# A streaming-encoder layer: gate row spread over the up-projection tiles, first weight products and DVE pages ahead of it

## The chip, the cores and the metric

The kernel runs on one core of one Trainium2 chip. Its metric is the device time of one execution in microseconds (us), the median of several runs. Five engines with an instruction stream each work side by side: TensorE (PE, matmuls), VectorE (DVE), ScalarE (ACT), GpSimd (POOL) and SyncE (SP). In this kernel SP issues the DMA transfers, in the order of its own stream: a transfer whose wait is not met holds all later ones back. A matmul reads its operands from on-chip memory (SBUF) and sums into one of the banks of PSUM; DVE and ACT read PSUM.

## The reference, cut to what matters

One layer on 1024 tokens of width 1024, all in float32. The attention half ends in an output projection with a gated residual; the channel half is a gated MLP of inner width 2816 with a causal convolution of width 3:

```
mod = silu(c) @ w_ada + b_ada;  sh_a, sc_a, g_a, sh_m, sc_m, g_m = split(mod, 6)
...
mixed = concat([o_mla, o_ca]) @ w_out
x = x + g_a * mixed
h = rmsnorm(x) * (1 + sc_m) + sh_m
u = causal_dwconv(h @ w_up, conv_w, conv_b)
gate, val = split(u, 2)
x = x + g_m * ((silu(gate) * val) @ w_down)
```

The row `g_m`, the last sixth of `mod`, is needed only where the down-projection's weights are multiplied by it.

## The kernel before, in words

A float32 product is made of three faster matmuls: each operand is split into a high part (ACT copies it to a shorter format) and a low part (DVE or POOL subtracts the high part from the original), and high x high, high x low and low x high are summed. Such a pair of 128x512 pieces is called a page when it belongs to the activations. The helpers `hi_of` (L75) and `lo_of` (L82) record all of these splits, so their rows all carry those two lines and are told apart by their tiles.

The part around the change has three stages.

*Output projection* (L873 to L901). For each of 8 blocks of 128 tokens: load `ol` (the attention output, transposed), the residual `x1` and a partial sum `pa`, split `ol`, 24 matmuls into a PSUM tile `op`, then DVE adds `pa` (L887), multiplies by the attention gate (L888); the residual add (L889) is on DVE for odd blocks and on POOL for even ones. The sum is stored (L890), squared and summed on ACT (L891), its inverse root made on POOL (L115, L116), and the block scaled in place on POOL (`scale_pool`, L71), which must wait until the store has read it. The tile `x1` has 6 buffers, so the loads of blocks 6 and 7 wait until PE has transposed blocks 0 and 1 for the last time.

*Pages.* `mod_T` turns four scaled blocks on PE (L858) and modulates them on ACT (L860). The first half of the tokens gives the pages `b11` and `b21` (four each). After block 7 the second half is done (L905 to L917): for each of four k, two `mod_T`, four subtractions on DVE (L908, L910, L913, L915) and five pages `t3`, `t1`, `b22`, `t2`, `t4`. ACT makes the five high parts; POOL makes the low parts of `t3`, `b22` and `t4`, DVE those of `t1` and `t2`. These pages, with the combinations of weights in `ff_tile`, are Winograd's form of a 2x2 block product: 7 products in place of 8.

*Up-projection* (`ff_tile`, L974), 22 tiles. A tile loads two raw weight pieces of 512 KB (`raw`, 3 buffers), forms on DVE the combinations of its quarters (L990, L992, L993, L1000), splits seven 128x512 pieces `wa` to `wg` (ACT high, POOL low, 7 buffers `ws`), and runs 7 products of 12 matmuls (L962 to L964), in the order wa with `b11`, wb with `b21`, wc with `t3`, wd with `t2`, we with `t1`, wf with `t4`, wg with `b22`. DVE adds the products up out of PSUM (L995 to L1002), then come the convolution (ACT L969, DVE L970, L971), the SiLU gate and a store. After tile 2 stands `gate_row` (L937): eight loads of 512 KB of `w_ada` through the same three `raw` buffers, eight multiply-adds over 128x1024 on DVE (L942, L944), the bias row (L455), two matmuls with a matrix of ones that sum over the partitions (L456) and two copies to `gmbc`.

*Down-projection* (from L1011): two halves of 22 steps of 24 matmuls, with weights multiplied by `gmbc` (L1024).

The order inside each engine's stream is not that of the source: the framework that builds the program reorders by its own estimate of times, engine by engine, and takes waits from the buffers.

Of the kernel before, what the change touches and what calls it, by code (L numbers as in the profile page):

```python
# [23 lines left out]
P = 128  # L24
D = 1024
# [37 lines left out]
def layer_kernel(ctx, tc, I, out):  # L63
# [809 lines left out]
    for t in range(NT):  # L873
        lo = gb.tile([P, 4, P], F32R, name=f"ol{t}", tag="ol", bufs=3)
        hi = gb.tile([P, 4, P], F32R, name=f"oh{t}", tag="oh", bufs=3)
        sp.dma_start(f32(lo[:]), oT_d[0:4, :, t * P:(t + 1) * P].rearrange("k p t -> p k t"))
        hi_of("a", hi[:], f32(lo[:]))
        lo_of("p", lo[:], f32(lo[:]), hi[:])
        x1 = tb.tile([P, D], F32, name=f"x1_{t}", tag="x1", bufs=6)
        sp.dma_start(x1[:], I["x"][t * P:(t + 1) * P, :])  # L880
# [6 lines left out]
        dve.tensor_tensor(pa[:], pa[:], pt[:], op=ADD)  # L887
        dve.tensor_tensor(pa[:], pa[:], gabc[:], op=MUL)  # L888
        (dve if t % 2 else pool).tensor_tensor(x1[:], x1[:], pa[:], op=ADD)  # L889
        sp.dma_start(x1_d[t], x1[:])  # L890
        act.activation(pa[:], x1[:], AF.Square, accum_out=ss2[:, t:t + 1])  # L891
        rsqrt_mean(r2[:, t:t + 1], ss2[:, t:t + 1], D)
        xn2[t] = x1
        scale_pool(x1[:], x1[:], r2[:, t:t + 1])
        if t % 4 == 3:
            h = t // 4
            if h == 0:
                for k in range(ND):
                    v0[k] = mod_T(k, 0)
                    bpage("b11" if k < 4 else "b21", k % 4, v0[k], "v" if k % 2 else "p")  # L900
# [4 lines left out]
    for k in range(4):  # L905
        b12, b22 = mod_T(k, 1), mod_T(k + 4, 1)
        t3 = tb.tile([P, 512], F32, name=f"t3_{k}", tag="v", bufs=11)
        dve.tensor_tensor(t3[:], b22[:], b12[:], op=SUB)  # L908
# [6 lines left out]
        dve.tensor_tensor(v0[k + 4][:], v0[k + 4][:], b22[:], op=SUB)  # L915
        bpage("t4", k, v0[k + 4], "p")
    tbp.__exit__(None, None, None)  # L917
    psB.__exit__(None, None, None)

    mlp = tc.tile_pool(name="mlp", bufs=1, side="right", reuse_waits="tile")
    mp = mlp.__enter__()
    psC = tc.tile_pool(name="psC", bufs=1, space=PSUM, reuse_waits="tile")
    ps3 = psC.__enter__()
    MB = {"raw": 3, "s": 5, "ws": 7, "c": 2, "u": 2}

    def mt(tag, shape, name, dt=F32):
        return mp.tile(list(shape), dt, name=name, tag=tag, bufs=MB[tag])  # L930

    def bank(tag, name, n=1):
        return ps3.tile([P, n * 512], F32, name=name, tag=tag, bufs=1)


    def gate_row():
        acc = mt("u", [P, D], "adacc5")  # L937
        for k in range(ND):
            w = mt("raw", [P, D], f"adaw5_{k}")
            sp.dma_start(w[:], I["w_ada"][k * P:(k + 1) * P, 5 * D:6 * D])  # L940
            if k == 0:
                dve.tensor_scalar(acc[:], w[:], cs[:, 0:1], None, op0=MUL)  # L942
            else:
                dve.scalar_tensor_tensor(acc[:], w[:], cs[:, k:k + 1], acc[:], op0=MUL, op1=ADD)  # L944
        for h in range(2):
            pt = bank("G", f"p_gm{h}")
            gate_bcast(pt[:], acc[:, h * 512:(h + 1) * 512], 5 * D + h * 512, 512, lambda n: mt("s", [P, 512], n))
            act.activation(gmbc[:, h * 512:(h + 1) * 512], pt[:], AF.Copy)

    def split(src, nm):
        w = mt("ws", [P, 2, 512], nm, F32R)
        hi_of("a", w[:, 0], src)
        lo_of("p", w[:, 1], src, w[:, 0])
        return w

    def product(pt, w, b):
        for k in range(4):
# [3 lines left out]
            pe.matmul(pt, sh, pg[:, 1], start=False, stop=False)  # L963
            pe.matmul(pt, sl, pg[:, 0], start=False, stop=(k == 3))  # L964

    def conv(c, ch):
# [3 lines left out]
        dve.scalar_tensor_tensor(u[:, 1:], c[:, :S - 1], pk[:, cv + 1:cv + 2], u[:, 1:], op0=MUL, op1=ADD)  # L970
# [3 lines left out]
    def ff_tile(j):  # L974
        raw = []
        for i in range(2):
            r = mt("raw", [P, D], f"wu{i}_{j}")
            sp.dma_start(r[:], I["w_up"][i * NF + j].rearrange("p k m -> p (k m)"))
            raw.append(r)
        a11, a12, a21, a22 = raw[0][:, :512], raw[0][:, 512:], raw[1][:, :512], raw[1][:, 512:]  # L980
        p1, p5, p6 = (bank(n, f"{n}_{j}") for n in ("p1", "p5", "p6"))
        p27, p34 = bank("p27", f"p27_{j}", 2), bank("p34", f"p34_{j}", 2)

        c = mt("c", [P, 7, 512], f"c{j}")
        product(p1[:], split(a11, f"wa{j}"), "b11")
        act.activation(c[:, 0], p1[:], AF.Copy)
        product(p27[:, :512], split(a12, f"wb{j}"), "b21")

        t3 = mt("s", [P, 512], f"ws3_{j}")
        dve.tensor_tensor(t3[:], a11, a21, op=SUB)  # L990
        product(p27[:, 512:], split(t3[:], f"wc{j}"), "t3")
# [3 lines left out]
        dve.tensor_tensor(c[:, 6], c[:, 0], p6[:], op=ADD)  # L995
        dve.tensor_tensor(c[:, 0::5][:, 0:2], c[:, 0::6][:, 0:2], p27[:].rearrange("p (a b) -> p a b", a=2), op=ADD)
# [121 lines left out]
```

## Time and profile before

| | us |
|---|---|
| median of 3 runs | 1493.73 (1491.92 to 1497.59) |
| the profiled execution, its own time | 1497.56 |
| its span in the profile | 1495.8 |
| PE busy | 1283.1 |
| DVE busy | 1037.7 |
| POOL busy | 841.8 |
| ACT busy | 617.5 |

Rows of the timeline give the start and the duration in us, the engine, the source line, the operation, what it writes `<-` what it reads, the shape, the count of merged instructions, and in brackets how long the engine had been idle before and what ended that. Rows of a table by stretches give, for each stretch, its length, each engine's busy time with the count of instructions, the granted TensorE clock (1.00 is full speed), the share of the DMA engines and the rate moved. Matmuls overlap: their spacing, not the printed duration, is their price.

### The profile page before, as it was taken

To read this page: it belongs to the slowest core of one execution; us is meant where nothing else is said; L and a number is where in the kernel's file an instruction comes from. 1 tells how busy PE (TensorE), PEld (TensorE's weight loads), DVE (VectorE), ACT (ScalarE), POOL (GpSimd) and SP (SyncE) were. 2 spreads that over 40 slices of the span, in tenths; PEclk is the share of its full clock that TensorE was granted. 3 is DMA by queue.
4 is the path that set the end of the run, shared out by engine and by line. 5 is a ranking of instruction groups with operands and counts; after the bars stand their busy time and mean duration, and the time that the engine had idled before them with its cause. 6 is when DMAs were issued, how large, how long until landed. Compare 5 with 4: busy or idle time off the path is not lost.

```text
span 1495.8 us, 20236 instructions
## 1 busy us (share of the span) xinstructions
PE 1283.1 (86%) x6836; PEld 1063.9 (71%) x6836; DVE 1037.7 (69%) x1710; ACT 617.5 (41%) x1190; POOL 841.8 (56%) x860
## 2 busy tenths in 40 slices
PE   3859989998968788876829769999999999999997
PEld 2759868976747666655617558888888887887885
DVE  6864786466768768863576658887787788556553
ACT  4454353343546545532444224444444443332331
POOL 4264453373799845443766146665565555665663
PEclk9979988998878899987958979999999999999999
DMA  7323656464512668778411242222222234446442
GB/s 275 134 70 73 135 121 143 116 134 102 124 49 53 145 144 167 163 156 287 149 74 57 71 143 82 85 85 85 85 85 84 77 129 169 148 148 234 154 141 99
DMA packets 217443, 185.94 MB, mean 124 GB/s; under 512 B 147958, under 2 KB 182906, under 8 KB 216316
## 3 DMA queue, kind: packets, MB, share of 16 engines
q1 hardware_dynamic: 217340, 184.66, 43.0%
q8 instruction: 54, 0.88, 0.2%
q14 instruction: 49, 0.40, 0.1%
HBM read 121.17 MB, written 28.84 MB: 100 GB/s over the span
## 4 chain that ended last, share of the span: by engine, by line
PE 48%; DMA 16%; DVE 13%; POOL 12%; issue 7%; ACT 2%; SPq 1%; DVEq 0%; POOLq 0%; ACTq 0%
PE p L964 7%; PE p L962 7%; PE p L963 7%; POOL wds L82 4%; DMA aw<-w_ada 4%; DMA PTm<-hlm 3%; PE sc L658 3%; PE dnp L1034 2%; PE dnp L1036 2%; PE dnp L1035 2%; DVE adacc L243 1%; DMA wu<-w_up 1%; PE ipv L150 1%; DVE aacc L430 1%; PE pvc L716 1%
## 5 line engine op out<-in xcount | busy, mean ns | idle before, releaser
L82 POOL TENSOR_TENSOR wds<-wd,wds 128x512 fp32r<-128x512 f32 x88 | 153.5, 1763 | 100.2 <-ACT wds L75 100.2
L1034 PE MATMUL dnp<-wds,g 128*128 128x512 f32 x308 | 119.9, 391 | 4.3 <-DVE xo L1042 2.4
L1024 DVE TENSOR_TENSOR wd<-wd,gmbc 128x1024 f32<-128x1024 f32 x44 | 69.4, 1578 | 77.7 <-DMA wd<-w_down 77.7
L1035 PE MATMUL dnp<-wds,g 128*128 128x512 f32 x308 | 119.7, 389 | 0.0
L1036 PE MATMUL dnp<-wds,g 128*128 128x512 f32 x308 | 118.5, 390 | 0.5 <-DVE g L82 0.5
L75 ACT ACTIVATE wds<-wd 128x512 fp32r<-128x512 f32 x88 | 54.6, 624 | 152.0 <-PE dnp L1036 149.6
L71 POOL TENSOR_SCALAR hlm<-Pm,rim 128x512 f16<-128x512 f32 (+4 forms) x88 | 61.7, 704 | 71.6 <-DMA PTm<-hlm 53.9
L703 DVE SCALAR_TENSOR_TENSOR hlm<-Pm,rim,hlm 128x512 f16<-128x512 f32 (+4 forms) x88 | 69.7, 795 | 31.7 <-POOL hlm L71 31.4
L71 POOL TENSOR_SCALAR hlc<-Pc,ric 128x640 f16<-128x640 f32 (+2 forms) x64 | 45.5, 713 | 77.9 <-DVE ric L686 38.7
L82 POOL TENSOR_TENSOR wc<-ws,wc 128x512 fp32r<-128x512 f32 x22 | 50.8, 2311 | 64.9 <-ACT wc L75 64.9
L82 POOL TENSOR_TENSOR wa<-wu,wa 128x512 fp32r<-128x512 f32 x22 | 35.9, 1633 | 91.1 <-ACT wa L75 91.1
L970 DVE SCALAR_TENSOR_TENSOR u<-c,pk,u 128x1023 f32<-128x1023 f32 x44 | 75.6, 1725 | 4.1 <-ACT u L969 4.1
L82 DVE TENSOR_TENSOR g<-gr,g 128x512 fp32r<-128x512 f32 x44 | 70.9, 1613 | 8.8 <-ACT g L75 8.8
L683 ACT ACTIVATE Pc<-sc,mc 128x640 f32<-128x640 f32 (+2 forms) x64 | 42.2, 659 | 83.6 <-DVE mc L673 66.9
L658 PE MATMUL sm<-mk,mq 96*128 96x512 f32 (+3 forms) x288 | 70.2, 378 | 7.0 <-ACT Pm L683 6.5
L716 PE MATMUL pvm<-PTm,vt 128*128 128x128 f16 x576 | 50.6, 242 | 29.4 <-DMA PTm<-hlm 25.3
L658 PE MATMUL sc<-k,q 64*128 64x512 f32 (+3 forms) x288 | 69.8, 370 | 5.6 <-ACT Pc L683 3.7
L430 DVE SCALAR_TENSOR_TENSOR aacc<-aw,cs,aacc 128x256 f32<-128x256 f32 x84 | 45.5, 541 | 41.8 <-DMA aw<-w_ada 41.2
L716 PEld LDWEIGHTS <-vt 128*128 128x128 f16 x576 | 41.2, 110 | 42.8 <-issue 40.0
L1034 PEld LDWEIGHTS dnp<-wds,g 128*128 128x128 f32 x308 | 57.8, 188 | 18.0 <-DVE xo L1042 3.3
L1036 PEld LDWEIGHTS dnp<-wds,g 128*128 128x128 f32 x308 | 57.8, 188 | 13.5 <-DVE g L82 1.4
L971 DVE SCALAR_TENSOR_TENSOR u<-c,pk,u 128x1022 f32<-128x1022 f32 x44 | 66.8, 1554 | 0.0
(352 smaller groups left out, 4350.8 us busy)
## 6 DMA issues: line engine op xcount, KB each, us to landing
wu<-w_up SPq DMA_DIRECT2D x44, 512.0 KB, 3.5
wd<-w_down SPq DMA_DIRECT2D x44, 512.0 KB, 3.5
aw<-w_ada SPq DMA_DIRECT2D x96, 128.0 KB, 2.3
g_d<-u SPq DMA_DIRECT2D x22, 512.0 KB, 2.6
gr<-g_d SPq DMA_DIRECT2D x44, 256.0 KB, 3.1
x<-x SPq DMA_DIRECT2D x16, 512.0 KB, 7.4
adaw<-w_ada_a SPq DMA_DIRECT2D x8, 1024.0 KB, 4.9
wq_r<-w_qk SPq DMA_DIRECT2D x32, 128.0 KB, 2.4
```

Source lines behind the costliest of these rows:

```text
L71: pool.tensor_scalar(o, i, s, 1.0, op0=MUL, op1=MUL)
L82: (pool if eng == "p" else dve).tensor_tensor(o, i, f32(hi), op=SUB)
L658: last = pe.matmul(s[:, c:c + w], qpg[rs_, a, q], kpgs[kh][rs_, b, ko:ko + w], start=(a == 0 and b == 0), stop=(a == 1))
L703: dve.scalar_tensor_tensor(hl[:, w:2 * w], pp, ri[:], hl[:, :w], op0=MUL, op1=SUB)
L716: last = pe.matmul(u.pv[:, c], u.vst(j), mov, start=(x == 0), stop=(x == len(todo) - 1))
L962: pe.matmul(pt, sh, pg[:, 0], start=(k == 0), stop=False)
L963: pe.matmul(pt, sh, pg[:, 1], start=False, stop=False)
L964: pe.matmul(pt, sl, pg[:, 0], start=False, stop=(k == 3))
L970: dve.scalar_tensor_tensor(u[:, 1:], c[:, :S - 1], pk[:, cv + 1:cv + 2], u[:, 1:], op0=MUL, op1=ADD)
L1034: pe.matmul(pts[t][n], sh, w[n][:, 0], start=(j == 0), stop=False)
L1035: pe.matmul(pts[t][n], sh, w[n][:, 1], start=False, stop=False)
L1036: pe.matmul(pts[t][n], sl, w[n][:, 0], start=False, stop=(j == NF - 1))
```

## The change

Four things are changed.

1. *Gate row.* `gate_row` becomes a generator that is advanced once after each tile from tile 2 on. It loads one block of 128 rows of `w_ada` as two 128x512 pieces into the five buffers `s` one step ahead, and sums it straight into `gmbc` with two DVE instructions per block (tiles 3 to 10). After two more steps come the bias, the two matmuls and the copies.
2. *First tile's head.* The loads of tile 0's weights and its first two products (wa with `b11`, wb with `b21`) are put ahead of the second half's pages. They sum into a PSUM tile of the output projection, and ACT copies both to a `raw` buffer `p12_0`. For this the buffers `raw` and a new pair `w2` (wa and wb of every tile, and `g` of the down-projection) are allocated in a pool of their own before the pages; `ws` shrinks from 7 to 5.
3. *Low parts.* All 20 low parts of the second half's pages are made by DVE (before: 8 by DVE, 12 by POOL).
4. *Blocks 6 and 7.* `x1` has 8 buffers in place of 6; for these two blocks the residual add and the scaling are on DVE.

In the streams that result, SP issues both weight loads of tile 0 ahead of the last load of `w_out` and of the residual loads, and the residual loads of blocks 6 and 7 directly behind the other six. PE's stream has tile 0's two products among the transposes after block 7's matmuls, and DVE's has the 36 instructions of the second half's pages in a row, with the first weight combination of tile 0 behind them.

```diff
-        x1 = tb.tile([P, D], F32, name=f"x1_{t}", tag="x1", bufs=6)
+        x1 = tb.tile([P, D], F32, name=f"x1_{t}", tag="x1", bufs=8)
...
-        (dve if t % 2 else pool).tensor_tensor(x1[:], x1[:], pa[:], op=ADD)
+        (dve if t % 2 or t > 5 else pool).tensor_tensor(x1[:], x1[:], pa[:], op=ADD)
...
-        scale_pool(x1[:], x1[:], r2[:, t:t + 1])
+        (dve if t > 5 else pool).tensor_scalar(x1[:], x1[:], r2[:, t:t + 1], 1.0, op0=MUL, op1=MUL)
...
-    MB = {"raw": 3, "s": 5, "ws": 7, "c": 2, "u": 2}
+    mlp0 = tc.tile_pool(name="mlp0", bufs=1, side="right", reuse_waits="tile")
+    mp = {"a": mlp0.__enter__()}
+    MB = {"raw": 3, "w2": 2, "s": 5, "ws": 5, "c": 2, "u": 2}
...
+    def ff_head(j, p1, p2):
+        raw = []
+        for i in range(2):
+            r = mt("raw", [P, D], f"wu{i}_{j}")
+            sp.dma_start(r[:], I["w_up"][i * NF + j].rearrange("p k m -> p (k m)"))
+            raw.append(r)
+        product(p1, split(raw[0][:, :512], f"wa{j}", "w2"), "b11")
+        product(p2[:, :512], split(raw[0][:, 512:], f"wb{j}", "w2"), "b21")
+        return raw, p1, p2
+
+    pre = ps2.tile([P, 1024], F32, name="op_0", tag="op", bufs=3)
+    head = ff_head(0, pre[:, :512], pre[:, 512:])
+    pc = mt("raw", [P, D], "p12_0")
+    act.activation(pc[:], pre[:], AF.Copy)
+    head = (head[0], pc[:, :512], pc[:, 512:])
     for k in range(4):
...
-        bpage("t3", k, t3, "p")
+        bpage("t3", k, t3, "v")
...
-        bpage("b22", k, b22, "p")
+        bpage("b22", k, b22, "v")
...
-        bpage("t4", k, v0[k + 4], "p")
+        bpage("t4", k, v0[k + 4], "v")
...
     def gate_row():
-        acc = mt("u", [P, D], "adacc5")
+        def load(k):
+            ws = [mt("s", [P, 512], f"adaw5_{k}{h}") for h in range(2)]
+            for h in range(2):
+                c = 5 * D + h * 512
+                sp.dma_start(ws[h][:], I["w_ada"][k * P:(k + 1) * P, c:c + 512])
+            return ws
+
+        nxt = load(0)
+        yield
         for k in range(ND):
-            w = mt("raw", [P, D], f"adaw5_{k}")
-            sp.dma_start(w[:], I["w_ada"][k * P:(k + 1) * P, 5 * D:6 * D])
+            cur, nxt = nxt, load(k + 1) if k + 1 < ND else None
+            for h in range(2):
+                acc = gmbc[:, h * 512:(h + 1) * 512]
...
+                    dve.scalar_tensor_tensor(acc, cur[h][:], cs[:, k:k + 1], acc, op0=MUL, op1=ADD)
+            yield
+        yield
...
+    gr_gen = gate_row()
     for j in range(NF):
-        ff_tile(j)
-        if j == 2:
-            gate_row()
+        if j:
+            head = ff_head(j, bank("p1", f"p1_{j}")[:], bank("p27", f"p27_{j}", 2)[:])
+        ff_tile(j, head)
+        if j >= 2:
+            next(gr_gen, None)
```

More of the change, by code (lines that the diff above doesn't have):

```diff
@@ L904, in layer_kernel, with split @@
     hpools.append(bp2.__enter__())
[L905 to L908, printed above, removed]
-        bpage("t3", k, t3, "p")
-        dve.tensor_tensor(b12[:], b12[:], v0[k][:], op=SUB)
-        bpage("t1", k, b12, "v")
-        bpage("b22", k, b22, "p")
-        dve.tensor_tensor(b22[:], b22[:], b12[:], op=SUB)
-        bpage("t2", k, b22, "v")
-        dve.tensor_tensor(v0[k + 4][:], v0[k + 4][:], b22[:], op=SUB)
-        bpage("t4", k, v0[k + 4], "p")
[L917 to L926, printed above, removed]
-    MB = {"raw": 3, "s": 5, "ws": 7, "c": 2, "u": 2}
-    def mt(tag, shape, name, dt=F32):
[L930 to L936, printed above, removed]
-        acc = mt("u", [P, D], "adacc5")
-        for k in range(ND):
-            w = mt("raw", [P, D], f"adaw5_{k}")
-            sp.dma_start(w[:], I["w_ada"][k * P:(k + 1) * P, 5 * D:6 * D])
[L941 to L953, printed above, removed]
+    mlp0 = tc.tile_pool(name="mlp0", bufs=1, side="right", reuse_waits="tile")
+    mp = {"a": mlp0.__enter__()}
+    MB = {"raw": 3, "w2": 2, "s": 5, "ws": 5, "c": 2, "u": 2}
+    def mt(tag, shape, name, dt=F32):
+        return mp["a" if tag in ("raw", "w2") else "b"].tile(list(shape), dt, name=name, tag=tag, bufs=MB[tag])
+    def split(src, nm, tag="ws"):
+        w = mt(tag, [P, 2, 512], nm, F32R)
         hi_of("a", w[:, 0], src)
@@ new lines, in layer_kernel @@
+    head = ff_head(0, pre[:, :512], pre[:, 512:])
+    pc = mt("raw", [P, D], "p12_0")
+    act.activation(pc[:], pre[:], AF.Copy)
+    head = (head[0], pc[:, :512], pc[:, 512:])
+    for k in range(4):
+        b12, b22 = mod_T(k, 1), mod_T(k + 4, 1)
+        t3 = tb.tile([P, 512], F32, name=f"t3_{k}", tag="v", bufs=11)
+        dve.tensor_tensor(t3[:], b22[:], b12[:], op=SUB)
+        bpage("t3", k, t3, "v")
+        dve.tensor_tensor(b12[:], b12[:], v0[k][:], op=SUB)
+        bpage("t1", k, b12, "v")
+        bpage("b22", k, b22, "v")
+        dve.tensor_tensor(b22[:], b22[:], b12[:], op=SUB)
+        bpage("t2", k, b22, "v")
+        dve.tensor_tensor(v0[k + 4][:], v0[k + 4][:], b22[:], op=SUB)
+        bpage("t4", k, v0[k + 4], "v")
@@ new lines, in layer_kernel, with bank, gate_row @@
+    tbp.__exit__(None, None, None)
+    psB.__exit__(None, None, None)
+    mlp = tc.tile_pool(name="mlp", bufs=1, side="right", reuse_waits="tile")
+    mp["b"] = mlp.__enter__()
+    psC = tc.tile_pool(name="psC", bufs=1, space=PSUM, reuse_waits="tile")
+    ps3 = psC.__enter__()
+    def bank(tag, name, n=1):
+        return ps3.tile([P, n * 512], F32, name=name, tag=tag, bufs=1)
+    def gate_row():
+        def load(k):
[6 more added lines that the diff above has]
+        yield
+        for k in range(ND):
+            cur, nxt = nxt, load(k + 1) if k + 1 < ND else None
+            for h in range(2):
+                acc = gmbc[:, h * 512:(h + 1) * 512]
+                if k == 0:
+                    dve.tensor_scalar(acc, cur[h][:], cs[:, 0:1], None, op0=MUL)
+                else:
+                    dve.scalar_tensor_tensor(acc, cur[h][:], cs[:, k:k + 1], acc, op0=MUL, op1=ADD)
+            yield
+        yield
+        for h in range(2):
+            acc = gmbc[:, h * 512:(h + 1) * 512]
+            pt = bank("G", f"p_gm{h}")
+            gate_bcast(pt[:], acc, 5 * D + h * 512, 512, lambda n: mt("s", [P, 512], n))
+            act.activation(acc, pt[:], AF.Copy)
@@ L972, in conv, with ff_tile @@
         return u
[L974 to L979, printed above, removed]
+    def ff_tile(j, head):
+        raw, p1, p2 = head
         a11, a12, a21, a22 = raw[0][:, :512], raw[0][:, 512:], raw[1][:, :512], raw[1][:, 512:]
-        p1, p5, p6 = (bank(n, f"{n}_{j}") for n in ("p1", "p5", "p6"))
-        p27, p34 = bank("p27", f"p27_{j}", 2), bank("p34", f"p34_{j}", 2)
+        p5, p6, p34 = bank("p5", f"p5_{j}"), bank("p6", f"p6_{j}"), bank("p34", f"p34_{j}", 2)
         c = mt("c", [P, 7, 512], f"c{j}")
-        product(p1[:], split(a11, f"wa{j}"), "b11")
-        act.activation(c[:, 0], p1[:], AF.Copy)
-        product(p27[:, :512], split(a12, f"wb{j}"), "b21")
+        if j:
+            act.activation(c[:, 0], p1, AF.Copy)
         t3 = mt("s", [P, 512], f"ws3_{j}")
         dve.tensor_tensor(t3[:], a11, a21, op=SUB)
-        product(p27[:, 512:], split(t3[:], f"wc{j}"), "t3")
+        p7 = p2[:, 512:] if j else bank("p1", "p7_0")[:]
+        product(p7, split(t3[:], f"wc{j}"), "t3")
         dve.tensor_tensor(a21, a21, a22, op=ADD)
@@ L994, in ff_tile @@
         product(p6[:], split(a11, f"wd_{j}"), "t2")
-        dve.tensor_tensor(c[:, 6], c[:, 0], p6[:], op=ADD)
-        dve.tensor_tensor(c[:, 0::5][:, 0:2], c[:, 0::6][:, 0:2], p27[:].rearrange("p (a b) -> p a b", a=2), op=ADD)
+        dve.tensor_tensor(c[:, 6], c[:, 0] if j else p1, p6[:], op=ADD)
+        if j:
+            dve.tensor_tensor(c[:, 0::5][:, 0:2], c[:, 0::6][:, 0:2], p2[:].rearrange("p (a b) -> p a b", a=2), op=ADD)
+        else:
+            dve.tensor_tensor(c[:, 0], p1, p2, op=ADD)
+            dve.tensor_tensor(c[:, 5], c[:, 6], p7, op=ADD)
         product(p5[:], split(a21, f"we{j}"), "t1")
@@ L1008, in ff_tile @@
         sp.dma_start(g_d[j], ug[:])
+    gr_gen = gate_row()
     for j in range(NF):
-        ff_tile(j)
-        if j == 2:
-            gate_row()
+        if j:
+            head = ff_head(j, bank("p1", f"p1_{j}")[:], bank("p27", f"p27_{j}", 2)[:])
+        ff_tile(j, head)
+        if j >= 2:
+            next(gr_gen, None)
     for h in range(2):
@@ L1027, in layer_kernel @@
             sp.dma_start(gr[:], g_d[j][:, h * 512:(h + 1) * 512])
-            g = mt("ws", [P, 2, 512], f"g{h}_{j}", F32R)
+            g = mt("w2", [P, 2, 512], f"g{h}_{j}", F32R)
             hi_of("a", g[:, 0], gr[:])
@@ L1046, in layer_kernel @@
     mlp.__exit__(None, None, None)
+    mlp0.__exit__(None, None, None)
     bp2.__exit__(None, None, None)
```

## The prediction

> **What bounds the kernel now.** I read the page's sums first, then a table by stretches, then the timeline at the two stretches where PE is idle, then the periodic part.
>
> ```profile
> span 1495.8 us, 20236 instructions
> PE 1283.1 (86%) x6836; PEld 1063.9 (71%) x6836; DVE 1037.7 (69%) x1710; ACT 617.5 (41%) x1190; POOL 841.8 (56%) x860
> ```
>
> ```profile
> core 0: us, PE busy (x) PEld busy (x) DVE busy (x) ACT busy (x) POOL busy (x), PEclk, DMA share, GB/s
> 684.00:744.00 60.00, 53.70 (x221) 42.35 (x222) 29.68 (x24) 19.41 (x34) 35.98 (x31) 0.90 0.59 212
> 744.00:787.00 43.00, 9.18 (x37) 6.10 (x37) 31.77 (x30) 23.52 (x40) 27.32 (x21) 0.54 0.23 86
> 849.00:874.00 25.00, 0.71 (x1) 0.50 (x2) 18.34 (x17) 4.58 (x5) 0.79 (x1) 0.59 0.50 170
> 874.00:1239.00 365.00, 365.00 (x1600) 300.90 (x1598) 292.25 (x244) 153.76 (x212) 221.67 (x137) 1.00 0.25 88
> ```
>
> From 874 to 1239 PE never rests: tiles 3 to 21 are bound by PE. It rests in two places: 744 to 787 (second half's pages) and 849 to 874 (gate row). The change touches both.
>
> ```profile
> 810.69 0.39 PE L962 MATMUL p<-b,wa 128*128 128x512 f32 x1
> 829.73 0.39 PE L962 MATMUL p<-b,wa 128*128 128x512 f32 x1
> 848.54 0.39 PE L964 MATMUL p<-b,wg 128*128 128x512 f32 x1
> 857.78 0.75 DVE L942 TENSOR_SCALAR adacc<-adaw,cs 128x1024 f32<-128x1024 f32 x1
> 863.61 3.92 DVE L944 SCALAR_TENSOR_TENSOR adacc<-adaw,cs,adacc 128x1024 f32<-128x1024 f32 x3 [2.43 <-DMA adaw<-w_ada]
> 868.38 1.28 DVE L944 SCALAR_TENSOR_TENSOR adacc<-adaw,cs,adacc 128x1024 f32<-128x1024 f32 x1 [0.85 <-DMA adaw<-w_ada]
> 872.50 0.63 ACT L75 ACTIVATE wa<-wu 128x512 fp32r<-128x512 f32 x1 [16.12 <-DMA wu<-w_up]
> 873.29 2.08 PE L456 MATMUL p_gm<-adacc,ones 128*128 128x512 f32 x2 [24.36 <-DVE adacc L455]
> 880.83 1.02 PE L456 MATMUL p_gm<-adacc,ones 128*128 128x512 f32 x2
> 881.29 0.80 PE L964 MATMUL p<-b,wb 128*128 128x512 f32 x1
> 896.22 0.39 PE L962 MATMUL p<-b,wa 128*128 128x512 f32 x1
> ```
>
> A tile takes 829.73 - 810.69 = 19.04 us, 0.227 per matmul. After tile 2 (848.54 + 0.23 = 848.77) PE waits 24.36 us for DVE's sum, which waits for `w_ada`; tile 3's weights come behind those eight loads (ACT idle 16.12).
>
> **The change part by part.**
>
> *Gate row.* From the end of tile 2 to the first matmul of tile 4 pass 896.22 - 848.77 = 47.45 us, 28.4 more than a tile. What stays on PE is the two sums over partitions: the second took 881.29 - 880.83 = 0.46 at full speed; with weight loads I put 1.2 for both. Gain 27.2. What it now costs lies on DVE and SP in tiles 3 to 10:
>
> ```profile
> 980.00:1200.00 220.00, 220.00 (x973) 182.15 (x972) 177.06 (x152) 92.79 (x126) 132.19 (x82) 1.00 0.23 82
> L970 DVE SCALAR_TENSOR_TENSOR u<-c,pk,u 128x1023 f32<-128x1023 f32 x23 | 41.8, 1816 | 0.0
> 1022.47 2.94 POOL L82 TENSOR_TENSOR wc<-ws,wc 128x512 fp32r<-128x512 f32 x1 [4.03 <-ACT wc L75]
> 1034.94 0.39 PE L962 MATMUL p<-t,wc 128*128 128x512 f32 x1
> 1029.20 0.33 SPq L978 DMA_DIRECT2D wu<-w_up  x1
> 1032.72 0.69 DVE L990 TENSOR_TENSOR ws<-wu,wu 128x512 f32<-128x512 f32 x1 [1.80 <-DMA wu<-w_up]
> ```
>
> DVE is busy 177.06/220 x 19.04 = 15.3 us of a tile, idle 3.7. The same kind of instruction over 1024 costs 1.28 where POOL stands still (868.38) and 1.82 beside POOL's splits (L970), so two of 512 cost 1.3 to 1.8 a tile: they fit. Behind them wait the next combination and its split, and wc's is done at 1022.47 + 2.94 = 1025.4 for a matmul at 1034.94: 9.5 us of slack. On SP stand two more loads of 256 KB a tile, one step ahead, between the two weight loads; a weight load takes 1032.72 - 1029.20 = 3.5 us and has the same slack. The bias rows and two ACT copies move with the sum. Direct cost 0; upper end below, under the rivals.
>
> The Trainium skill ("SBUF — State Buffer", section "Who interferes with whom") says that a DVE instruction with two SBUF inputs contends with a POOL instruction that reads SBUF, and that the later one stops for the whole of the other. The two prices above, 1.28 and 1.82, agree in kind. The rule gives a rival (below).
>
> *Blocks 6 and 7, out-projection.*
>
> ```profile
> x_d<-x SPq DMA_DIRECT2D x8, 512.0 KB, 2.7
> 680.00:700.00 20.00, 15.78 (x57) 12.39 (x58) 5.97 (x8) 5.02 (x8) 5.08 (x4) 0.76 0.97 346
> 697.53 2.35 DVE L887 TENSOR_TENSOR pa<-pa,op 128x1024 f32<-128x1024 f32 x2 [3.39 <-PE op L152]
> 707.23 0.80 PE L150 MATMUL op<-wo,oh 128*128 128x512 f32 x1 [3.61 <-ACT oh L75]
> 741.48 0.40 PE L152 MATMUL op<-wo,ol 128*128 128x512 f32 x1
> 744.21 0.81 SPq L880 DMA_DIRECT2D x<-x  x2
> 749.04 2.83 DVE L889 TENSOR_TENSOR x<-x,pa 128x1024 f32<-128x1024 f32 x1 [0.45 <-DMA x<-x]
> 755.00 2.22 POOL L71 TENSOR_SCALAR x<-x,r 128x1024 f32<-128x1024 f32 x2
> 758.00 1.45 ACT L860 ACTIVATE hv<-ht_ps,modT 128x512 f32<-128x512 f32 x2 [3.91 <-PE ht_ps L858]
> ```
>
> Now: block 7's matmuls end at 741.9, its residual is issued only at 744.21, the add runs 749.04 to 751.87, store, scaling to 757.2, first modulation 758.00. Then: behind 741.9 stand on DVE L887, block 6's scaling, L888 and the add. With L887's 2.35 for two, 1.2 each, and 0.75 for a scaling on DVE (L942 above; POOL's take 1.1), that is 4.35, so the add ends at 746.25. The store takes 2.7 (to 748.95; square and inverse root lie beside it), the scaling 0.75, the transposes 0.4: first modulation at 750.1, 7.9 earlier. Up to 1 more where POOL's splits of `b21` lie beside the adds.
>
> Against it: four more loads of 512 KB (tile 0's weights, blocks 6 and 7) enter a stretch whose DMA engines are 97% busy at 346 GB/s: 2.1 MB / 346 GB/s = 6.1 us of transfer. They delay the last piece of `w_out`; PE bridges that with block 2's first products, so blocks 0 and 1 end some 12 matmuls, about 3 us, later, and L887 (697.53) with them. Behind it come the residual adds, then on ACT, in order, the squares and the split of block 3, for which PE already waits 3.61 us (707.23). That wait grows by 0 to 6.1; I take 2, since part of the 3 is hidden by the adds' own time. First modulation at 752.1. The head's two splits on POOL fall where POOL awaits DVE and cost nothing.
>
> *Pages.*
>
> ```profile
> L82 DVE TENSOR_TENSOR t<-hv,t x8: 678/685/1750, 763.6 to 785.5; 128x512 fp32r<-128x512 f32 x8
> L82 POOL TENSOR_TENSOR t<-hv,t x4: 1593/1686/1711, 765.6 to 786.2; 128x512 fp32r<-128x512 f32 x4
> 763.61 0.68 DVE L82 TENSOR_TENSOR t<-hv,t 128x512 fp32r<-128x512 f32 x1
> 764.21 0.68 DVE L915 TENSOR_TENSOR hv<-hv,hv 128x512 f32<-128x512 f32 x1
> 786.72 0.80 PE L962 MATMUL p<-b,wa 128*128 128x512 f32 x1 [16.45 <-ACT wa L75]
> 789.61 0.79 PE L964 MATMUL p<-b,wa 128*128 128x512 f32 x1 [0.82 <-POOL wa L82]
> ```
>
> Now 24 DVE instructions, 0.68 alone and up to 1.75 beside POOL, share the work with 12 of POOL at 1.6: from 758.00 to 786.72, 28.7 us. Then 36 on DVE with POOL empty: spaced 0.60 (763.61 to 764.21) to 0.69, 21.6 to 24.8; I take 23.4. Before them two modulations, 1.5; ACT's 20 high parts at 0.63, 8 modulations and the copy of `p12_0` need some 20 us and run beside, but the two engines pass work to and fro: 0.8. Then wc's combination 0.65 and high part 0.65. Sum 27.0: PE starts wc at 779.1. The gain here is only 1.7, because DVE does all the work alone; the gain is in the instruction price.
>
> *Head.* Tile 0 took 810.69 - 786.72 = 23.97 us, 4.9 over the 19.04: a slow clock (0.54 in the table) at first and 0.82 for the first low part. After: 60 matmuls x 0.227 = 13.6, and 4.5 for the same start, 18.1. The 24 matmuls ahead lie in PE's idle time after 744. Tile 0 ends at 779.1 + 18.1 = 797.2, 13.5 before 810.69.
>
> *Lag.* `p12_0` holds one of three `raw` buffers, so tile 1's loads wait for tile 0's splits, where now they are there before. By the spacing above they land some 4 us later than in the periodic part, inside the 9.5 of slack; I take 1.5 for this and for DVE's fuller stream, ends 0 and 7.
>
> *Sum.* 27.2 + 13.5 - 1.5 = 39.2. The profiled execution, 1497.56, becomes 1458.4; it stands 3.8 above the median, so 1493.73 - 39.2 = 1454.5, say 1455.
>
> **The rivals.**
>
> *DVE becomes the bound in tiles 3 to 10.* By a full stop behind a POOL split, 1.6 each, two blocks cost 2 x (0.65 + 1.6) = 4.5 a tile against 3.7 idle: 0.8 over in eight tiles, 6 to 7 us. Time 1461. The skill's rule above speaks for it; L970's 1.82 beside POOL, 0.54 more and not 1.6, speaks against.
>
> *The low parts do not get cheap.* If DVE's 36 instructions keep the old mean, about 1.1 (0.68 to 1.75 in the rows), they take 40 us in place of 23.4: the change does not do what it says, tile 0 ends 3 later than now, and only the gate row's gain is left, 39.2 - 16.6 = 22.6: 1471. For it: long links between ACT and DVE. Against: in the new order POOL has nothing between `b21` and wc's low part.
>
> *Slower.* The three `raw` buffers stay late in every tile: a weight load waits behind a block's load and the store on SP, and the split misses its matmul. From the 9.5 us of slack on, PE loses the rest in every tile; 21 tiles at 2.2 us would eat the 39 and give 1501 from there. For it: ACT's 16.12 us wait for weights behind `w_ada`. Against: the periodic part issues both loads within a tile and DVE waits only 1.80 for them.
>
> *No change*: a mixture, say a DMA crowd of 6 and 1.5 a tile lost; no single row supports it.
>
> **How the numbers follow.** Forecast 0.63 (own range 1446 to 1460), DVE bound 0.12, dear low parts 0.13, slower 0.07, near no change 0.03, more gain than forecast 0.02. The range reaches to the dear low parts, 1472 with rounding, and down by the unspent ends (2 for the crowd, 1.8 for the 0.60 spacing, 1.5 lag, about 3 if the slow start is shorter) to 1446. The 0.5% bound, 7.5 us, is about what a measurement here can tell from no change. Faster 0.90, same 0.03, slower 0.07.
>
> **What would show it.** After: no PE gap over 2 us between tile 0 and the down-projection; the `gmbc` sums at 0.65 to 0.9 each; POOL empty and DVE at about 0.68 through the pages; the residual add of block 7 without a wait for its load; a longer wait than 3.61 before block 3. The prediction is wrong if the tiles run over 19.04, if DVE's low parts stay above 1, or if block 3's wait passes 10.

## The result, and the profile after

| | us |
|---|---|
| before, median of 4 runs | 1494.70 (1491.92 to 1497.59) |
| after, median of 4 runs | 1462.41 (1460.86 to 1464.36) |
| ratio | 0.9771, 95% interval 0.9750 to 0.9792 |
| profiled execution: before, after | 1497.56, 1464.36 |
| its span: before, after | 1495.8, 1462.2 |

The change makes the kernel 32.3 us faster by the medians and 33.6 by the spans. The forecast was a gain of 39.2 and 1455, so 5.6 us of it are missing by the spans and 6.9 by the medians. They are found in the tiles in which the gate row is summed.

The sums of the page, after:

```profile
span 1462.2 us, 20198 instructions
PE 1278.0 (87%) x6836; PEld 1058.7 (72%) x6836; DVE 1013.6 (69%) x1734; ACT 611.4 (42%) x1190; POOL 823.0 (56%) x845
```

The table by stretches, after (columns as before: length, busy time of each engine, granted clock, DMA share, GB/s):

```profile
684.00:744.00 60.00, 52.21 (x217) 42.02 (x218) 28.68 (x24) 19.99 (x35) 39.27 (x34) 0.88 0.70 249
744.00:779.00 35.00, 13.72 (x63) 9.74 (x61) 29.51 (x44) 24.17 (x40) 4.70 (x5) 0.69 0.04 15
833.84:852.88 19.04, 19.04 (x85) 15.77 (x84) 14.82 (x15) 6.86 (x11) 10.66 (x8) 1.00 0.31 111
912.29:932.27 19.98, 19.33 (x85) 15.69 (x84) 15.82 (x16) 7.79 (x12) 11.59 (x8) 1.00 0.29 106
972.20:991.24 19.04, 19.04 (x86) 15.77 (x84) 14.81 (x15) 8.03 (x12) 11.32 (x8) 1.00 0.23 83
1203.58:1462.22 258.64, 241.41 (x1057) 197.50 (x1055) 151.95 (x105) 77.47 (x129) 148.28 (x86) 0.98 0.45 156
```

The 24 us hole of PE at the gate row is gone. What is new stands in the fourth row: a tile of 19.98 us. Tile 3 (third row) and tile 10 (fifth row) take 19.04, PE's own time. Between them, tile 4 takes 0.40 more than that and tiles 5 to 9 some 0.93 more each.

The timeline of the changed kernel from the out-projection to the steady part:

```profile
708.96 0.80 PE L150 MATMUL op<-wo,oh 128*128 128x512 f32 x1 [6.53 <-ACT oh L75]
742.10 0.39 PE L152 MATMUL op<-wo,ol 128*128 128x512 f32 x1
745.09 0.76 DVE L894 TENSOR_SCALAR x<-x,r 128x1024 f32<-128x1024 f32 x1 [1.34 <-DMA x_d<-x]
747.01 2.18 DVE L889 TENSOR_TENSOR x<-x,pa 128x1024 f32<-128x1024 f32 x1
751.95 1.12 DVE L894 TENSOR_SCALAR x<-x,r 128x1024 f32<-128x1024 f32 x1 [2.15 <-DMA x_d<-x]
753.49 1.45 ACT L860 ACTIVATE hv<-ht_ps,modT 128x512 f32<-128x512 f32 x2 [2.08 <-PE ht_ps L858]
754.97 0.69 DVE L947 TENSOR_TENSOR t<-hv,hv 128x512 f32<-128x512 f32 x1 [1.30 <-ACT hv L860]
777.83 0.68 DVE L1015 TENSOR_TENSOR ws<-wu,wu 128x512 f32<-128x512 f32 x1
779.29 0.79 PE L924 MATMUL p<-t,wc 128*128 128x512 f32 x1 [14.12 <-ACT wc L75]
779.32 1.53 POOL L82 TENSOR_TENSOR wc<-ws,wc 128x512 fp32r<-128x512 f32 x1 [26.80 <-ACT wc L75]
795.76 0.39 PE L924 MATMUL p<-b,wa 128*128 128x512 f32 x1
852.88 0.39 PE L924 MATMUL p<-b,wa 128*128 128x512 f32 x1
875.87 0.47 PE L924 MATMUL p<-b,wb 128*128 128x512 f32 x1 [0.67 <-DVE c L1023]
991.24 0.39 PE L924 MATMUL p<-b,wa 128*128 128x512 f32 x1
1010.28 0.39 PE L924 MATMUL p<-b,wa 128*128 128x512 f32 x1
1014.01 0.47 PE L924 MATMUL p<-b,wb 128*128 128x512 f32 x1 [0.85 <-DVE c L1023]
1051.26 0.39 PE L924 MATMUL p<-b,wa 128*128 128x512 f32 x1
```

Four things are to be seen. The first modulation of the second half comes at 753.49 (758.00 before). DVE runs through its 36 instructions in 777.83 - 754.97 = 22.9 us while POOL stands still for 26.80. Tile 0 ends at 795.76, 14.9 earlier than before. And in a tile with sums PE waits at the first matmul of wb (875.87), because DVE has not yet read the PSUM bank `p27` of the tile before (L1023).

*Where the 33.6 us are.* Tile 0 ends 810.69 - 795.76 = 14.93 earlier. Of this, 1.35 lies ahead of the out-projection, whose first matmul came at 682.75 after 684.10 (it varies from 682.1 to 689.6 among the traces); 13.6 lies behind it. The hole of the gate row gives 28.41 (47.45 less a tile). Tiles 4 to 9 give back 0.40 + 5 x 0.93 = 5.1. Tiles 12 and 13, with the two sums over partitions, take 1051.26 - 1010.28 = 40.98, 2.90 over two tiles. In the first experiment below, where wb does not wait, the same two tiles take 39.85, so the sums cost 1.8 and the further wait of wb for L1023 (1014.01) 1.1. The down-projection takes 258.64 after 256.84. Its instructions are the same in all kernels here, and only the buffers of `g` differ (`ws` before, `w2` after). With the buffers of before it takes 256.8 and, in the run of the new gate row alone, 260.5; with those of after 256.4 to 261.2, apart from 253.4 in the kernel with a fourth `raw` buffer. So these 1.8 are not put down to the change. 14.93 + 28.41 - 5.1 - 2.9 - 1.8 = 33.6.

### The profile page after: what moved, and what is told of

It reads as the page before. It is cut to its first block, busy times and chain, and to the rows that moved or that the text cites. A ratio compares the mean times of both kernels' runs of the same rounds, so it can differ in the third digit from the quotient of the medians.

```text
span 1462.2 us, 20198 instructions
## 1 busy us (share of the span) xinstructions
PE 1278.0 (87%) x6836; PEld 1058.7 (72%) x6836; DVE 1013.6 (69%) x1734; ACT 611.4 (42%) x1190; POOL 823.0 (56%) x845
## 4 chain that ended last, share of the span: by engine, by line
PE 39%; DMA 17%; DVE 15%; POOL 13%; issue 12%; ACT 3%; SPq 1%; DVEq 0%; POOLq 0%; ACTq 0%
POOL wds L82 5%; DMA aw<-w_ada 5%; PE p L924 4%; PE p L926 4%; PE p L925 4%; DMA wu<-w_up 3%; DMA PTm<-hlm 3%; PE sc L658 2%; PE dnp L1067 2%; PE dnp L1069 2%; PE dnp L1068 2%; PE sm L658 2%; DVE adacc L243 2%; DVE aacc L430 1%; DVE u L1002 1%
## 5 line engine op out<-in xcount | busy, mean ns | idle before, releaser
L82 POOL TENSOR_TENSOR wc<-ws,wc 128x512 fp32r<-128x512 f32 x22 | 65.4, 2972 | 137.8 <-ACT wc L75 137.8
L1015 DVE TENSOR_TENSOR ws<-wu,wu 128x512 f32<-128x512 f32 x22 | 30.7, 1396 | 76.2 <-DMA wu<-w_up 76.2
L1036 ACT ACTIVATE u<-u 128x1024 f32<-128x1024 f32 x22 | 23.4, 1063 | 132.1 <-DVE u L1002 132.1
L1000 ACT ACTIVATE u<-c,pk 128x1024 f32<-128x1024 f32 x44 | 52.3, 1236 | 56.2 <-DVE c L1032 56.2
L1069 PEld LDWEIGHTS dnp<-wds,g 128*128 128x128 f32 x308 | 57.8, 188 | 17.7 <-DVE g L82 5.7
```

The costliest lines, as they stand in the source:

```text
L82: (pool if eng == "p" else dve).tensor_tensor(o, i, f32(hi), op=SUB)
```

## The experiments

Theory A, formed from the trace after, is a ring of waits. These rows are one turn of it, in a tile with sums:

```profile
917.43 1.30 POOL L82 TENSOR_TENSOR wf<-wu,wf 128x512 fp32r<-128x512 f32 x1
918.75 0.33 SPq L933 DMA_DIRECT2D wu<-w_up  x1
922.25 1.48 DVE L1015 TENSOR_TENSOR ws<-wu,wu 128x512 f32<-128x512 f32 x1 [3.92 <-DMA wu<-w_up]
923.64 2.31 DVE L1001 SCALAR_TENSOR_TENSOR u<-c,pk,u 128x1023 f32<-128x1023 f32 x1
925.87 0.68 DVE L1018 TENSOR_TENSOR wu<-wu 128x512 f32<-128x512 f32 x1
926.47 1.27 DVE L1001 SCALAR_TENSOR_TENSOR u<-c,pk,u 128x1023 f32<-128x1023 f32 x1
927.67 0.74 DVE L988 SCALAR_TENSOR_TENSOR gmbc<-adaw,cs,gmbc 128x512 f32<-128x512 f32 x1
928.33 1.27 DVE L1002 SCALAR_TENSOR_TENSOR u<-c,pk,u 128x1022 f32<-128x1022 f32 x1
929.53 0.74 DVE L988 SCALAR_TENSOR_TENSOR gmbc<-adaw,cs,gmbc 128x512 f32<-128x512 f32 x1
929.70 1.07 ACT L1036 ACTIVATE u<-u 128x1024 f32<-128x1024 f32 x1 [7.38 <-DVE u L1002]
930.19 1.27 DVE L1002 SCALAR_TENSOR_TENSOR u<-c,pk,u 128x1022 f32<-128x1022 f32 x1
931.36 3.61 POOL L82 TENSOR_TENSOR wc<-ws,wc 128x512 fp32r<-128x512 f32 x1 [6.49 <-ACT wc L75]
931.38 0.68 DVE L1019 TENSOR_TENSOR wu<-wu,wu 128x512 f32<-128x512 f32 x1
931.99 1.21 DVE L1037 TENSOR_TENSOR u<-u,u 128x1024 f32<-128x1024 f32 x1
933.12 0.68 DVE L1030 TENSOR_TENSOR wu<-wu 128x512 f32<-128x512 f32 x1
934.92 1.27 POOL L82 TENSOR_TENSOR wd<-wu,wd 128x512 fp32r<-128x512 f32 x1
936.16 1.29 POOL L82 TENSOR_TENSOR we<-wu,we 128x512 fp32r<-128x512 f32 x1
937.41 1.29 POOL L82 TENSOR_TENSOR wf<-wu,wf 128x512 fp32r<-128x512 f32 x1
938.73 0.33 SPq L933 DMA_DIRECT2D wu<-w_up  x1
```

SP can issue the second weight load only when POOL has made wf's low part, which frees its `raw` buffer (917.43 + 1.30 = 918.73; issued 918.75). The load lands 3.50 later and lets DVE start the next tile (922.25). DVE works without a break to the end of L1030 at 933.80. On the way ACT, whose SiLU had waited 7.38 for the convolution, makes the high part of wc behind it, and so lets POOL begin at 931.36; but POOL's low part of wc ends only 1.2 after DVE's run. wd, we and wf take 3.7 more, and the next load leaves at 938.73. The turn is 938.73 - 918.75 = 19.98, the tile's time to the hundredth, and no PE instruction is in it. Both sums (0.66 each, by the starts) lie in DVE's part: without them the turn would be 18.66, under PE's 19.04.

The trace shows this turn too. The last sums stand at 947.64 and 949.50, and the loads behind them leave 18.65 apart:

```profile
958.70 1.59 SPq L933 DMA_DIRECT2D wu<-w_up  x2
977.35 1.58 SPq L933 DMA_DIRECT2D wu<-w_up  x2
996.00 0.33 SPq L933 DMA_DIRECT2D wu<-w_up  x1
```

The turn after these is 19.68 again (the next load leaves at 1015.68). In it DVE adds the two bias rows of the gate row (L455, 0.67 each) between the instructions of the convolution, and wb's wait of 0.85 in tile 12 follows.

Theory B is that the two `w_ada` loads per tile delay the weight loads. Theory C is the rival of the prediction: DVE has too little time in a tile.

### The sums moved into DVE's wait

```diff
+            with tc.issue_after(last[k + 1].ins):
                 for h in range(2):
...
-        dve.tensor_tensor(c[:, 1:3], c[:, 4:6], p34[:].rearrange("p (a b) -> p a b", a=2), op=ADD)
+        last[j] = dve.tensor_tensor(c[:, 1:3], c[:, 4:6], p34[:].rearrange("p (a b) -> p a b", a=2), op=ADD)
```

> The two gate-row sums of a tile are queued on DVE behind the last sum of products of a tile, where DVE then waits 3.9 us for the weight load; loads, SP order and arithmetic stay. Theory A (ring of waits: second weight load -> weight combination -> conv -> second weight combination on DVE -> POOL's low parts -> buffer free -> next load, into which the two sums put 1.3 us): tiles 4 to 9 return from 19.98 to 19.04 us, 5.1 us less in all, about 1457.3 where the changed kernel takes 1462.4. Theory B (the w_ada loads delay the weight loads): tiles stay at 19.98, time as the changed kernel. Theory C (DVE has too little time in a tile, wherever the sums stand): as B.

Measured: 1455.24 us (1454.73 to 1458.83), ratio to before 0.9740 (0.9724 to 0.9755). All tiles up to 11 take 19.04. Its timeline and its table by stretches (in this kernel the sum of products is L1035, the gate sum L991, the weight combination L1018):

```profile
909.16 1.22 DVE L1035 TENSOR_TENSOR c<-c,p 128x1024 f32<-128x1024 f32 x1 [0.50 <-PE p L926]
910.30 2.57 DVE L991 SCALAR_TENSOR_TENSOR gmbc<-adaw,cs,gmbc 128x512 f32<-128x512 f32 x2
914.05 1.72 DVE L1018 TENSOR_TENSOR ws<-wu,wu 128x512 f32<-128x512 f32 x1 [1.19 <-DMA wu<-w_up]
```

```profile
908.96:928.00 19.04, 19.04 (x85) 15.77 (x84) 17.21 (x15) 7.90 (x11) 10.79 (x8) 1.00 0.30 110
```

Theories B and C fall: the loads are the same, and DVE is busier in the faster tile (17.21 of 19.04 against 15.82 of 19.98). The pair of sums even costs more here, 2.57 beside POOL's splits, but it stands in a wait for the load of which 1.19 is left.

### The sums made thin, the loads kept

```diff
                 else:
+                    acc = acc[:, :8]
-                    dve.scalar_tensor_tensor(acc, cur[h][:], cs[:, k:k + 1], acc, op0=MUL, op1=ADD)
+                    dve.scalar_tensor_tensor(acc, cur[h][:, :8], cs[:, k:k + 1], acc, op0=MUL, op1=ADD)
```

> All loads and waits of the changed kernel, but seven of the eight blocks are summed over 8 of each 512 columns only, so that DVE's instructions cost next to nothing (part of the gate row is left out). Theories A and C: tiles 4 to 9 at 19.04, about 1457. Theory B: still 19.98, about 1462.

Measured: 1457.34 us (1454.43 to 1461.16), ratio 0.9747 (0.9729 to 0.9766); tiles 4 to 9 at 19.04. Theory B falls a second time.

### The sums kept, the loads left out

```diff
-            cur, nxt = nxt, load(k + 1) if k + 1 < ND else None
+            cur = nxt
```

Each sum is tied behind the same convolution instruction of DVE as in the changed kernel.

> All sums, in the same places of DVE's stream as in the changed kernel, but all eight read the first block of w_ada, so seven of eight pairs of loads are gone (the gate row is that of a repeated block). Theories A and C: tiles 4 to 9 stay at about 19.98, time about 1462. Theory B: 19.04, about 1457.

Measured: 1464.28 us (1461.99 to 1470.87), ratio 0.9800 (0.9777 to 0.9822). The tiles stay long without the loads, here at 79 to 80 GB/s in place of 106:

```profile
934.65:954.63 19.98, 19.29 (x86) 15.69 (x84) 15.81 (x16) 7.80 (x12) 11.60 (x8) 1.00 0.22 80
```

### One sum per tile over 16 tiles

```diff
-        for k in range(ND):
-            cur, nxt = nxt, load(k + 1) if k + 1 < ND else None
-            for h in range(2):
+        for n in range(2 * ND):
+            k, h = n // 2, n % 2
+            cur, nxt = nxt, load(n + 1) if n + 1 < 2 * ND else None
...
             yield
```

> The changed kernel with one 128x512 sum per tile over 16 tiles in place of two over eight. Ring of waits: without sums it takes about 19.98 - 2 x 0.66 = 18.66 us, so one sum makes 19.32, 0.28 over PE's 19.04 in 16 tiles = 4.5, less the lead of 2.4 us that the changed kernel shows before its tiles grow (8 x 0.94 = 7.5 against 5.1 lost): 2.1 lost in place of 5.1, about 1459. If a tile with any sum is disturbed as a whole: 16 x 0.94 less 2.4 = 12.6 lost, about 1470.

Measured: 1459.73 us (1459.02 to 1463.99), ratio 0.9763 (0.9741 to 0.9784). The tiles stay at 19.04 up to tile 10 and then turn to 19.3; the sum over 19.04 is 1.9 us, where 2.1 was expected. One of them:

```profile
1042.79:1062.10 19.31, 19.31 (x86) 15.69 (x84) 14.98 (x15) 7.79 (x12) 10.94 (x8) 1.00 0.26 96
```

This is the ring's own arithmetic: 18.66 + 0.66 = 19.32. At first a tile costs nothing, since the loads are some 2 us ahead of PE and this lead is used up at 0.28 a tile: POOL's low parts of wc start 19.31 apart from tile 3 on (848.76, 868.07, 887.38), while PE's tiles still take 19.04.

### A fourth raw buffer

The kernel of the experiment before last (sums kept, loads left out), with one more buffer:

```diff
-    MB = {"raw": 3, "w2": 2, "s": 5, "ws": 5, "c": 2, "u": 2}
+    MB = {"raw": 4, "w2": 2, "s": 3, "ws": 5, "c": 2, "u": 2}
```

> The kernel with all sums and seven of eight pairs of loads left out, with a fourth raw buffer (and three buffers s in place of five, for room): the sums stay between the instructions of the convolution, but a weight load no longer waits for the low parts of the tile just before. Ring of waits: tiles 4 to 9 return from 19.98 to 19.04, some 5 us less than that kernel, about 1459 (the down-projection may lose by the fewer s buffers). Theory C (DVE has too little time in a tile): 19.98 stays, 1464.

Measured: 1474.70 us (1471.80 to 1477.88), ratio 0.9854 (0.9825 to 0.9883): a clear miss. Tiles of 19.8 to 23.0, irregular:

```profile
927.93:949.28 21.35, 19.32 (x85) 15.70 (x84) 19.77 (x16) 7.89 (x11) 12.31 (x8) 1.00 0.22 74
```

The buffer also changed the order in DVE's stream: the weight combination and the sums of products now stand ahead of the convolution. DVE is busy 19.77 of 21.35 with the same instructions that took 15.8 above. Here DVE is close to being the bound. That the ring closes at the `raw` buffer is therefore read from the rows of the ring, from its 18.65 without sums and its 19.31 with one, and not shown by taking the buffer's wait away.

### The parts one by one

The changed kernel with the gate row of before in its old place:

```diff
+        if j == 2:
+            gate_row()
-        if j >= 2:
-            next(gr_gen, None)
```

> The changed kernel with the gate row of before: eight loads and eight full sums in one piece after tile 2. It leaves the head, the pages and blocks 6 and 7. By the prediction's terms 13.5 of 39.2 us stay: about 1480; by the changed kernel's trace, 14.9 at the end of tile 0 less 1.8 lost at the start of the down-projection: 1481 to 1482. The weights of tile 3 still wait behind the eight loads, so PE's gap of 24 us is back.

Measured: 1484.31 us (1483.28 to 1484.77), ratio 0.9925 (0.9912 to 0.9939), a gain of 11.3. Its trace has tile 0 ending at 794.95, 15.7 earlier than before, and the end of tile 21 15.8 earlier; its down-projection took 259.4. So the head, the pages and blocks 6 and 7 are together worth 13.2 by spans, 11.3 by medians.

The kernel before with the new gate row alone:

```diff
+    gr_gen = gate_row()
     for j in range(NF):
         ff_tile(j)
-        if j == 2:
-            gate_row()
+        if j >= 2:
+            next(gr_gen, None)
```

> The kernel before with the gate row of the changed kernel and nothing else of it. By the prediction's term 27.2 us faster: about 1468. By the ring of waits, if it is as tight in the kernel before (seven buffers ws in place of five and two): 28.4 for PE's gap, less 2.9 for the two sums over partitions as measured in the changed kernel, less 5.1 for tiles 4 to 9 at 19.98: 20.4 faster, about 1475.

Measured: 1478.49 us (1474.61 to 1482.57), ratio 0.9888 (0.9852 to 0.9924), a gain of 17.8 with an interval of 11 to 22. By the trace the 21 tiles after tile 0 take 405.0 us after 428.3, a gain of 23.2, between the two expectations of 20.4 and 27.2. The ring is as tight here (tiles of 19.98 and 19.94), but it is first felt three tiles later, for a loss of 2.3 in place of 5.1, because the work on the weights starts further ahead: in tile 3 wc's low part is done 7.0 us ahead of its matmul, in the changed kernel 4.2, and in both traces the tiles grow once this lead is down to 3.7.

The low parts of `t3`, `b22` and `t4` back on POOL:

```diff
-        bpage("t3", k, t3, "v")
+        bpage("t3", k, t3, "p")
...
-        bpage("b22", k, b22, "v")
+        bpage("b22", k, b22, "p")
...
-        bpage("t4", k, v0[k + 4], "v")
+        bpage("t4", k, v0[k + 4], "p")
```

> The changed kernel with the low parts of t3, b22 and t4 back on POOL, as before: 24 DVE and 12 POOL instructions in place of 36 on DVE. Theory D (the prediction's: the two engines slow each other, so sharing is worth nothing): the pages take 1.7 (prediction's 28.7 against 27.0) to 2.9 us longer (against the 25.8 measured), 1464 to 1465 where the changed kernel takes 1462.4. Theory E (DVE's 36 instructions are the path, POOL would take 12 of them off it): up to 12 x 0.6 = 7 us shorter, about 1455.

Measured: 1469.52 us (1468.93 to 1472.17), ratio 0.9822 (0.9799 to 0.9846), 7 slower than the changed kernel by the medians (5 slower than its second measurement below). Groups of DVE and POOL during the pages, and the start of wc (all of DVE's groups there cost 681 to 684 ns each in the changed kernel):

```profile
L82 DVE TENSOR_TENSOR t<-hv,t 128x512 fp32r<-128x512 f32 x8 | 8.0, 1006 | 1.7 <-ACT t L75 1.7
L82 POOL TENSOR_TENSOR b<-hv,b 128x512 fp32r<-128x512 f32 x5 | 7.7, 1532 | 3.9 <-ACT b L75 3.9
L952 DVE TENSOR_TENSOR hv<-hv,hv 128x512 f32<-128x512 f32 x4 | 5.9, 1483 | 0.0
```

```profile
785.26 0.79 PE L924 MATMUL p<-t,wc 128*128 128x512 f32 x1 [18.33 <-ACT wc L75]
```

From the last matmul of the out-projection to wc pass 42.4 us, in the changed kernel 779.29 - 742.10 = 37.2. Theory D has the right sign and too small a size; theory E falls.

Blocks 6 and 7 as before:

```diff
-        x1 = tb.tile([P, D], F32, name=f"x1_{t}", tag="x1", bufs=8)
+        x1 = tb.tile([P, D], F32, name=f"x1_{t}", tag="x1", bufs=6)
...
-        (dve if t % 2 or t > 5 else pool).tensor_tensor(x1[:], x1[:], pa[:], op=ADD)
+        (dve if t % 2 else pool).tensor_tensor(x1[:], x1[:], pa[:], op=ADD)
...
-        (dve if t > 5 else pool).tensor_scalar(x1[:], x1[:], r2[:, t:t + 1], 1.0, op0=MUL, op1=MUL)
+        pool.tensor_scalar(x1[:], x1[:], r2[:, t:t + 1], 1.0, op0=MUL, op1=MUL)
```

> The changed kernel with six x1 buffers, block 6's residual add and the scaling of blocks 6 and 7 on POOL, as before. By the prediction 7.9 us less the crowd of loads: first modulation 5.9 later; by the changed kernel's trace (753.49 against 758.00 before) 4.5 later: 1467 to 1468. If the gain of this part is eaten by the crowd of loads: no difference, 1462.

Measured: 1465.92 us (1464.63 to 1466.90), ratio 0.9794 (0.9772 to 0.9817), 3.5 slower than the changed kernel by the medians, with intervals that overlap. In its trace two effects oppose each other: the stretch from the out-projection's last matmul to wc is 5.5 longer (42.65), and the out-projection itself is shorter, 55.3 us from its first matmul to its last where the other traces have 56.6 to 59.5.

### Changed kernel, moved sums and late loads side by side

> The changed kernel as it is, beside the next ones on the same chip: 1462, tiles 4 to 9 at 19.98 us.

> The sums behind the last sum of products, as in the first experiment, now beside the changed kernel: 5 to 7 us less than it, about 1456.

The third kernel has the moved sums, and in addition:

```diff
+    with tc.issue_after(ol5):
+        head = ff_head(0, pre[:, :512], pre[:, 512:])
-    head = ff_head(0, pre[:, :512], pre[:, 512:])
...
+        with tc.issue_after(ol5) if t > 5 else ExitStack():
+            sp.dma_start(x1[:], I["x"][t * P:(t + 1) * P, :])
-        sp.dma_start(x1[:], I["x"][t * P:(t + 1) * P, :])
```

> The kernel with the sums in DVE's wait, and in addition tile 0's weight loads and the residual loads of blocks 6 and 7 queued on SP behind the load of ol of block 5, so that they no longer lie ahead of the transfers of the first blocks. If the crowd of loads causes the longer wait before block 3 (6.53 against 3.61 before): that wait falls by 2 to 2.9 us and the time with it, about 1453. If something else does: no change, about 1456.

| | median us | runs | ratio to before (95%) |
|---|---|---|---|
| changed kernel | 1464.47 | 1461.12 to 1466.94 | 0.9787 (0.9763 to 0.9810) |
| sums in DVE's wait | 1460.26 | 1457.01 to 1464.43 | 0.9762 (0.9738 to 0.9786) |
| and late loads | 1455.89 | 1453.41 to 1460.56 | 0.9737 (0.9713 to 0.9761) |

The moved sums gain 4.2 by the medians on the same chip, though the runs overlap. Their trace has all tiles up to 11 at 19.04 once more: from the start of tile 1 to the end of tile 21 pass 401.6 us, in the changed kernel beside it 407.5 and in its first trace 407.8, a gain of 5.9 to 6.2. The same kernel had 1455.24 in the first session, so medians of two sessions differ by up to 5 us, and a gain of this size is better read from the tiles. The late loads bring block 3's wait back:

```profile
707.33 0.80 PE L150 MATMUL op<-wo,oh 128*128 128x512 f32 x1 [3.62 <-ACT oh L75]
```

So the crowd of loads did cause the longer wait. But from the out-projection's first matmul to wc pass 94.8 us, with the early loads 94.4 beside it, and 93.4 to 96.5 in the other traces with the same pages, blocks and `raw` buffers. Of the 2.9 us, the out-projection is 0.6 shorter (57.3 after 58.0), and the stretch from its end to wc is 1.0 longer (37.4 after 36.5). The 4.4 us between the medians lie in no stretch that this edit touches, and the runs overlap: unresolved.

## Why the prediction was right and where it was wrong

The direction and the two large terms held. The time of 1462.4 is 7 us above the forecast of 1455, and outside the forecast's own range of 1446 to 1460; it lies inside only because the range was drawn up to 1472 for the dear low parts. Most of the signs named came: sums at 0.74, POOL empty with DVE at 0.68, block 7's add without a wait for its load, a longer wait before block 3, no wait of PE over 2 us. But the first sign of being wrong, tiles over 19.04, came as well.

*Blocks 6 and 7: mis-sized, and the time was nearly met in part by luck.* First modulation at 752.1 was forecast, 753.49 came, in an execution whose out-projection began 1.35 earlier than before. From the end of block 7's matmuls to this modulation 8.2 was forecast (741.9 to 750.1) and 11.0 came (742.5 to 753.49). DVE waits 1.34 for block 6's store before it scales that block (row 745.09), which the working put at nothing; the final add took 2.18 beside POOL in place of 1.2 (up to 1 more was allowed for), and the scaling of block 7 1.12 in place of 0.75. The wait of 2.15 for block 7's store (row 751.95) is as the working had it. Block 3's wait grew by 2.92, where 2 was taken from 0 to 6.1. Undoing the part cost 1.4 (from the out-projection's first matmul to the end of tile 0, 114.4 against 113.0) to 3.5 us (medians), not 5.9: the net of this part was put too high.

*Pages: right in time, for the right reason, mis-sized in worth.* 25.8 from the first modulation to wc, 27.0 forecast; DVE's price was 0.68 at a spacing of 0.60, and POOL stood still. But sharing with POOL costs 5 to 7 us and not 1.7: with POOL at work most of DVE's groups rise to 1.0 to 1.5, around the 1.1 that the rival "the low parts do not get cheap" took. In the changed kernel POOL had nothing to do there, as was argued against this rival.

*Head: right, with the slow start put too high.* Tile 0 takes 795.76 - 779.29 = 16.5 after the start of wc, 18.1 forecast; the start cost 2.9 over the 13.6, not 4.5. These three sum to 795.76 against 797.2; the errors of 1.4, -1.2 and -1.6 cancel in part.

*Gate row: 27.2.* The hole gave 28.41 as read. The two sums over partitions cost 1.8, not 1.2.

*"They fit", "Direct cost 0" and "Lag" (1.5): the step that failed.* The cost is 5.1 + 1.1 = 6.2, and the moved sums got back as much (407.8 to 401.6). DVE's 3.7 us idle per tile were taken as room, and the slack was read at wc's matmul (9.5). The idle time was DVE's wait for the weight load, a part of the ring, and the ring had 19.04 - 18.66 = 0.38 to spare. The bias rows, also at "direct cost 0", went into the same turn. The sums' own price was right (0.74, within 0.65 to 0.9).

*The rival "DVE becomes the bound in tiles 3 to 10"* gave 1461 and 6 to 7 us, close to what came, but by another mechanism, so that its nearness is luck. In the changed kernel no sum stops behind a split (0.74 each); where they do stop (2.57 for two, in the moved version) they cost nothing. The rule of the Trainium skill ("SBUF — State Buffer", "Who interferes with whom") is seen at another place: POOL's low part of wc, 1.27 to 1.3 alone for its like, lasts 3.61 while three DVE instructions with two SBUF inputs run (931.38 to 933.80): it stops for all three and not for one instruction alone. It lengthens the ring; it does not make DVE the bound.

*The rival "raw buffers stay late in every tile"* named the buffers rightly, but its loss is bounded by the sums: tiles without them return to 19.04.

## What to carry to other kernels

Idle time of an engine in a periodic stretch is room only if nothing waits for that engine's next event: follow the buffer that is freed last through load, engines and back to its release, add up that turn, and compare it with the period. Work put into the turn costs in full as soon as the turn passes the period; here the same work, put just ahead of the engine's longest wait, cost nothing, even at a higher price each. A loss of this kind starts late, after the lead of the loads is spent, so a short look at the first tiles does not show it.

## What the runs showed of the hardware

DVE's 128x512 instruction with two SBUF inputs took 0.68 us with POOL empty. Beside POOL's splits, the same group took up to 1.48 on average in the experiment with POOL's low parts, and POOL's own 1.53 to 1.61. Giving 12 of 36 such instructions to the second engine made the stretch 5 us longer.

After 14.12 us of waiting, PE's first matmuls of wc (row 779.29) came at slow spacing, at a granted clock of 0.51 for 5.1 us (779.29 to 784.42); tile 0's remaining 60 matmuls took 16.5 in place of 13.6, so this start cost 2.9, and not the 4.5 read from before.
